# A depthwise convolution split into even and odd columns, and low parts of weights moved from GpSimd to VectorE

## The chip, the core and the metric

The kernel runs on one core of a Trainium2 chip. The metric is the device time of one execution in microseconds; the median of three runs of the kernel before is 1464.91 us (1461.34 to 1465.78). TensorE multiplies matrices, VectorE and GpSimd work element by element, ScalarE applies functions, and SyncE issues the transfers from and to device memory. In the profile they are PE, DVE, POOL, ACT and SP.

## What is computed

One layer of a streaming encoder on 1024 positions of 1024 channels, all in fp32: a convolution branch and a stick-breaking attention branch, both from one input projection, merged by sigmoid gates, an output projection, and a SwiGLU feed-forward part. The change lies in the convolution branch:

```python
u = jax.nn.glu(conv_in, axis=-1)                       # 512 channels: value times sigmoid of gate
u = causal_depthwise_conv(u, conv_dw_w, conv_dw_b)     # 31 taps along the positions, one filter per channel
u = jax.nn.silu(layernorm(u, conv_ln_g, conv_ln_b))    # normalised over the channels
conv_out = jnp.einsum('bsc,cd->bsd', u, w_conv_branch) + b_conv_branch
...
merged = jax.nn.sigmoid(g_conv) * conv_out + jax.nn.sigmoid(g_att) * att_out
mix = jnp.einsum('bsd,de->bse', merged, w_out)
```

## The kernel before

**Matmuls in two parts.** Every fp32 matrix is split into a high part, rounded to the type that TensorE multiplies in one pass, and a low part, the rest. A product is three matmuls: high by high, high by low, low by high. `load_w` (lines 64 to 72) does it for a tile of weights: SyncE loads the raw tile into one of two buffers, ScalarE makes the high part `wh` (line 70), and GpSimd subtracts it from the raw tile for the low part `wl` (line 71). A few early calls name another engine for the subtraction. `dense_T` (lines 82 to 90) makes one product of 128 output channels by 512 positions: first the matmuls with the high weights (lines 77 and 78), then those with the low weights (line 80).

**The convolution.** Channels lie on the 128 partitions and positions run along the free dimension, so the 512 channels are four blocks. `load_glu` clears the first 30 columns of a tile `u`; `glu_chunk` makes half of its 1024 positions: for "g" ScalarE writes the sigmoid of the gate into it, for "a" VectorE multiplies the value, read from PSUM, by it. `dw_ops` (lines 444 to 464) lists the work of one block: one pass over 1024 columns that multiplies by the first tap and adds the bias (`first`), 30 passes that each add one more tap (`tap`, line 453), and a sum over blocks on GpSimd (`total`, line 459).

**The order of work.** Up to the feed-forward part the program is a list, and a planner lays out each engine's queue from it when the program is built: of what is ready by its reckoning it takes what comes first in the program. On the chip each queue runs in that order. Line 505 writes the order of the mixing stage: "t" is a gate of the attention branch and the product that it gates, "g" and "a" are gate and value of a convolution block (2 and 3 here; 0 and 1 were made during attention), "c" is a gate of the convolution branch. `next_w` loads the weights of a step when the step before it begins, into two pairs of buffers; `next_branch` does it for the narrower weights of the branch products. `pump(n)` issues n steps of the convolution, alternately from the two oldest blocks that are not done, after each half of a step; `pump(1000)` issues what is left. Eight PSUM banks serve the products; a product of "t" keeps its bank until VectorE has multiplied it by the gate (line 541). Eight tiles `sgt` hold gates.

Behind the convolution (lines 574 to 613) the channel mean comes from a matmul with a constant matrix `avg` (`spread`, line 563), then squares, variance, and the normalised value in high and low parts `yH` and `yL`. TensorE makes the first "c" gates meanwhile. The convolution branch's products follow (`conv_out`), the merge is split into parts, and the output projection (lines 662 to 684) begins with eight weight tiles loaded through the two raw buffers.

Of the kernel before, what the change touches and what calls it, by code (L numbers as in the profile page):

```python
# [7 lines left out]
F32 = mybir.dt.float32  # L8
# [3 lines left out]
ALU = mybir.AluOpType  # L12
# [3 lines left out]
P = 128  # L16
S = 1024
# [3 lines left out]
HALF = 512  # L21
CONV_W = 31
NCB = 4
# [4 lines left out]
SGT = 8  # L28
# [4 lines left out]
VG, VF, VLG, VLB, VDB, VBB = 0, 8, 16, 20, 24, 28  # L33
# [4 lines left out]
def layer_kernel(ctx, tc, x, vecs, dww, gains, ident_d, mask_d, wv, wi, wbr, wo, wu, wdq, wd, out):  # L38
# [3 lines left out]
    def pool(name, bufs=1, **kw):  # L42
        return tc.tile_pool(name=name, bufs=bufs, reuse_waits="tile", **kw)
# [17 lines left out]
    hH = big.tile([P, NK, S], F32R, name="hH")  # L61
    hL = big.tile([P, NK, S], F32R, name="hL")

    def load_w(src, pl=None, bufs=2, n=1024, sub=None):
        pl = pl or wst
        raw = wst.tile([P, 1024], F32, name="wraw", tag="wraw", bufs=2)[:, 0:n]
        SP.dma_start(out=raw, in_=src)
        wh = pl.tile([P, n], F32R, name="wh", tag="wh", bufs=bufs)
        wl = pl.tile([P, n], F32R, name="wl", tag="wl", bufs=bufs)
        A.activation(out=wh, in_=raw, func=AF.Copy)  # L70
        (sub or G).tensor_tensor(out=wl, in0=raw, in1=wh.bitcast(F32), op=ALU.subtract)  # L71
        return wh, wl

    def mm3(ps, steps, first=True, last=True):
# [282 lines left out]
    us = []  # L357

    def load_glu(cb, what):
        wts[what] = load_w(wi[{"g": 4, "a": 0, "t": 28}[what] + cb])  # L360
        if what == "g":
            u = w4("u")
            G.memset(u[:, 0:CONV_W - 1], 0.0)
            us.append(u)

    def glu_chunk(cb, what, c, bank):
        ps = bank("psg")
        dense_T(wts[what], c, ps)
        dst = us[cb][:, CONV_W - 1 + c * HALF:CONV_W - 1 + (c + 1) * HALF]
        if what == "g":  # L370
            A.activation(out=dst, in_=ps, func=AF.Sigmoid)
        else:
            V.tensor_tensor(out=dst, in0=ps, in1=dst, op=ALU.mult)
# [55 lines left out]
    def bank(nm):  # L429
        return ps8.tile([P, HALF], F32, name=nm, tag="d")  # L430

    with pool("mix") as mp:
        ones = mp.tile([P, P], F32, name="ones")
        avg = mp.tile([P, P], F32, name="avg")
        G.memset(ones, 1.0)
        G.memset(avg, 1.0 / 512.0)
        attHL = []
        accs = []
        merged = []
# [1 line left out]
        turn = [0]  # L441
        csums = []

        def dw_ops(cb):
            acc = arp.tile([P, S], F32, name="acc", tag="ar", bufs=4)
            accs.append(acc)
            u = us[cb]

            def first():
                V.tensor_scalar(out=acc, in0=u[:, 0:S], scalar1=dw[:, cb, 0:1], scalar2=vec[:, VDB + cb:VDB + cb + 1], op0=ALU.mult, op1=ALU.add)  # L450

            def tap(kk):
                V.scalar_tensor_tensor(out=acc, in0=u[:, kk:kk + S], scalar=dw[:, cb, kk:kk + 1], in1=acc, op0=ALU.mult, op1=ALU.add)  # L453

            def total():
                if cb == 1:
                    csums.append(w4("csum")[:, 0:S])
                if cb in (1, 2):
                    G.tensor_tensor(out=csums[0], in0=accs[0] if cb == 1 else csums[0], in1=acc, op=ALU.add)

            ops = [(first, ())]
            for kk in range(1, CONV_W):
                ops.append((tap, (kk,)))
            dwq.append(ops + [(total, ())])

        def pump(n):
# [31 lines left out]
        def gate_sig(w, c):  # L498
            pg = bank("pg")
            dense_T(w, c, pg)  # L500
            sgt = mp.tile([P, HALF], F32, name="sgt", tag="sgt", bufs=SGT)
            A.activation(out=sgt, in_=pg, func=AF.Sigmoid)
            return sgt

# [17 lines left out]
        for pr in range(4):  # L522
            att_split(pr)
            if pr < 2:
                dw_ops(pr)
                pump(2)
        for kind, j in order:
            if kind == "c":
                break
            if (kind, j) == ("t", 2):  # L530
                pump(12)
            w = next_w()
            if kind == "t":
                w2 = next_branch()
                mg = mp.tile([P, S], F32, name="mg", tag="mg", bufs=8)
                for c in range(2):
                    cs = slice(c * HALF, (c + 1) * HALF)
                    sgt = gate_sig(w, c)
                    pb = bank("pb")
                    dense_T(w2, c, pb, attHL, 4)  # L540
                    V.tensor_tensor(out=mg[:, cs], in0=pb, in1=sgt, op=ALU.mult)
                    pump(8)
                merged.append(mg)
            else:
                wts[kind] = w
                for c in range(2):
                    glu_chunk(j, kind, c, bank)
                    pump(4)
                if kind == "a":
                    dw_ops(j)  # L550
        pump(1000)
# [28 lines left out]
        for cb in range(NCB):  # L580
# [4 lines left out]
            A.activation(out=sq, in_=accs[cb], func=AF.Square)  # L585
            sqs.append(sq)
            if cb == 1:
                G.tensor_tensor(out=sqs[1], in0=sqs[0], in1=sqs[1], op=ALU.add)
        V.tensor_tensor(out=sqs[3], in0=sqs[2], in1=sqs[3], op=ALU.add)
        V.tensor_tensor(out=sqs[3], in0=sqs[1], in1=sqs[3], op=ALU.add)  # L590
        gate_half(0, 1)
# [637 lines left out]
```

## Time and profile before

| | |
|---|---|
| median of three runs | 1464.91 us |
| the profiled execution | 1465.04 us |
| its span, from the first to the last instruction | 1463.2 us |
| mean granted clock of TensorE | 0.984 of full speed |
| TensorE busy | 1374.1 us, 94% |
| VectorE busy | 1057.3 us, 72% |
| ScalarE, GpSimd busy | 528.6 us and 282.3 us |

Shares of busy time are averages over stages that have different limits. The attention runs to about 350 us, the mixing stage with the convolution to about 690, the output projection and its norms to about 810, and the feed-forward part fills the rest. A granted clock of 1.00 is 2.4 GHz and 0.50 is 1.2 GHz. Durations of consecutive instructions on VectorE overlap a little, so that the pitch from start to start is shorter than the length of one.

### The profile page before, as it was taken

Reading aid. Unit: us, or ns where it says so; the run is one execution under the profiler, and the core shown is the slowest. Engines: PE = TensorE matmul, PEld = TensorE weight load, DVE = VectorE, ACT = ScalarE, POOL = GpSimd, SP = SyncE. Lnnn points to the kernel's source line nnn. Section 1 sums busy time; section 2 is a strip of 40 time slices with the busy share of each in tenths; the row PEclk is TensorE's granted clock in tenths of the full one; section 3 lists DMA queues with packets and bytes.
Section 4 is the critical chain, followed back from the end, with each engine's and each line's share of the span. In section 5 each row is a group of like instructions: output and inputs, shape, how many; then the busy total and the mean of one; then the engine's idle time right before and its main releaser. Section 6 shows DMA issues by size and latency. Waiting matters only on the chain.

```text
span 1463.2 us, 17209 instructions
## 1 busy us (share of the span) xinstructions
PE 1374.1 (94%) x6412; PEld 1126.8 (77%) x6412; DVE 1057.3 (72%) x1385; ACT 528.6 (36%) x863; POOL 282.3 (19%) x301
## 2 busy tenths in 40 slices
PE   6988998998999979999999799999999998999987
PEld 6866787777888757887787588888888887888875
DVE  5498878776999996325348899888877785644564
ACT  5466656553111104323325223222222222633450
POOL 2134323332324232322306200000000000000130
PEclk9999999999999989999999899999999999999999
DMA  6001001101111110212522155444444445965273
GB/s 221 23 26 40 22 23 32 42 30 36 45 49 52 43 44 22 65 43 81 172 87 94 65 198 184 174 157 158 143 149 162 166 137 178 371 230 177 89 272 100
DMA packets 62403, 160.97 MB, mean 110 GB/s; under 512 B 6384, under 2 KB 17904, under 8 KB 62320
## 3 DMA queue, kind: packets, MB, share of 16 engines
q1 hardware_dynamic: 62032, 158.83, 32.2%
q8 instruction: 50, 0.82, 0.2%
q10 hardware_dynamic: 288, 1.05, 0.2%
q14 instruction: 33, 0.27, 0.1%
HBM read 117.65 MB, written 40.11 MB: 108 GB/s over the span
## 4 chain that ended last, share of the span: by engine, by line
PE 66%; DVE 22%; issue 5%; ACT 3%; DMA 2%; POOL 2%; SPq 0%; DVEq 0%; POOLq 0%; ACTq 0%
PE m L914 28%; PE md L914 12%; DVE acc L453 11%; PE pg L77 2%; PE pg L78 2%; PE pg L80 2%; DVE R L260 2%; DVE R L255 2%; PE po L670 1%; PE po L669 1%; PE po L668 1%; DVE aL L321 1%; DVE R L257 1%; PE av L291 1%; PE pb L78 1%
## 5 line engine op out<-in xcount | busy, mean ns | idle before, releaser
L71 POOL TENSOR_TENSOR wl<-wraw,wh 128x1024 fp32r<-128x1024 f32 (+1 forms) x58 | 141.0, 2438 | 248.7 <-ACT wh L70 145.7
L453 DVE SCALAR_TENSOR_TENSOR acc<-u,dw,acc 128x1024 f32<-128x1024 f32 x120 | 176.9, 1531 | 0.3
L914 PE MATMUL m<-t,wh 128*128 128x512 f32 x528 | 134.8, 397 | 4.4 <-ACT wh L914 3.0
L914 PE MATMUL m<-hH,wh 128*128 128x512 f32 x328 | 130.6, 398 | 8.8 <-ACT wh L776 8.8
L914 PE MATMUL md<-wl,wh 128*128 128x512 f32 x308 | 122.5, 398 | 9.5 <-DVE wl L914 9.5
L914 PE MATMUL m<-hL,wh 128*128 128x512 f32 x328 | 129.9, 396 | 0.0
L914 PEld LDWEIGHTS m<-t,wh 128*128 128x128 f32 x528 | 100.0, 190 | 29.0 <-ACT wh L914 3.4
L914 PE MATMUL md<-wh 128*128 128x512 f32 x308 | 122.0, 396 | 0.0
L914 ACT ACTIVATE c<-c 128x512 f32<-128x512 f32 x44 | 27.8, 633 | 244.4 <-DVE c L914 244.4
L914 POOL TENSOR_TENSOR dc<-dc,gpo 128x512 f32<-128x512 f32 x4 | 5.1, 1301 | 541.4 <-ACT junk L914 541.4
L70 ACT ACTIVATE wh<-wraw 128x1024 fp32r<-128x1024 f32 (+1 forms) x60 | 56.5, 945 | 144.4 <-PE pg L78 50.7
L77 PE MATMUL pg<-hH,wh 128*128 128x512 f32 x256 | 101.5, 396 | 0.0
L78 PE MATMUL pg<-hL,wh 128*128 128x512 f32 x256 | 100.0, 391 | 0.0
L914 PE MATMUL md<-wh,wl 128*128 128x512 f32 x308 | 98.8, 395 | 0.0
L914 PE MATMUL m<-hH,wl 128*128 128x512 f32 x328 | 89.2, 393 | 0.0
L914 PEld LDWEIGHTS m<-hH,wh 128*128 128x128 f32 x328 | 62.2, 190 | 23.7 <-ACT wh L776 9.2
L914 PEld LDWEIGHTS md<-wl,wh 128*128 128x128 f32 x308 | 58.9, 191 | 24.5 <-DVE wl L914 11.8
L914 DVE TENSOR_TENSOR wl<-ra,wh 128x1024 fp32r<-128x1024 f32 (+1 forms) x42 | 48.4, 1153 | 38.1 <-ACT wh L914 38.0
L914 PEld LDWEIGHTS m<-hL,wh 128*128 128x128 f32 x328 | 62.2, 190 | 14.1
L914 PEld LDWEIGHTS m<-hH,wl 128*128 128x128 f32 x328 | 61.6, 188 | 14.3
L914 PE MATMUL m<-t,wl 128*128 128x512 f32 x264 | 70.7, 390 | 0.0
L914 DVE TENSOR_TENSOR u<-m,u 128x512 f32<-128x512 f32 x66 | 45.4, 688 | 33.5 <-PE m L914 32.1
(226 smaller groups left out, 3303.2 us busy)
## 6 DMA issues: line engine op xcount, KB each, us to landing
ra<-act SPq DMA_DIRECT2D x35, 512.0 KB, 6.8
wraw<-in_wi SPq DMA_DIRECT2D x32, 512.0 KB, 3.5
rg<-in_wu SPq DMA_DIRECT2D x23, 512.0 KB, 4.4
ru<-in_wu SPq DMA_DIRECT2D x22, 512.0 KB, 5.3
q<-in_wdq SPq DMA_DIRECT2D x22, 512.0 KB, 6.1
wsum<-q SPq DMA_DIRECT2D x22, 512.0 KB, 2.6
act<-sa SPq DMA_DIRECT2D x44, 256.0 KB, 2.7
rb<-wsum SPq DMA_DIRECT2D x20, 512.0 KB, 8.7
```

What stands on the lines that cost most here:

```text
L70: A.activation(out=wh, in_=raw, func=AF.Copy)
L71: (sub or G).tensor_tensor(out=wl, in0=raw, in1=wh.bitcast(F32), op=ALU.subtract)
L77: PE.matmul(ps, lhsT=lh, rhs=rh, start=(first and j == 0), stop=False)
L78: PE.matmul(ps, lhsT=lh, rhs=rl, start=False, stop=False)
L80: PE.matmul(ps, lhsT=ll, rhs=rh, start=False, stop=(last and j == n - 1))
L255: V.tensor_tensor_scan(out=R[:, 3:3 + n][:, ::-1], data0=d, data1=d, initial=1.0, op0=ALU.mult, op1=ALU.bypass)
L257: V.tensor_tensor(out=R[:, 4:3 + n], in0=sg[:, 0:n - 1], in1=R[:, 4:3 + n], op=ALU.mult)
L260: V.tensor_tensor_scan(out=R[:, 4:4 + n][:, ::-1], data0=d, data1=d, initial=carry, op0=ALU.mult, op1=ALU.bypass)
L291: PE.matmul(av, lhsT=vt[j][:, hh, :], rhs=aL[:, jj, :], start=False, stop=(j == 2 * m + 1))
L321: V.tensor_tensor(out=flat[1][:, 0:n * P], in0=tpf, in1=flat[0][:, 0:n * P].bitcast(F32), op=ALU.subtract)
L453: V.scalar_tensor_tensor(out=acc, in0=u[:, kk:kk + S], scalar=dw[:, cb, kk:kk + 1], in1=acc, op0=ALU.mult, op1=ALU.add)
L914: return lambda *a, **k: tc.keep_in_program_order(fn(*a, **k))
```

## The change

**The convolution.** `u` is kept as two halves, the even columns and the odd ones, each with its own cleared part, and `glu_chunk` writes them so, reading PSUM by every second column. With even and odd taps as two filters, three half-length filters make both halves of the output: the even taps on the even columns (16 taps, `p0`), the odd taps on the odd columns (15, `p1`), and the sums of neighbouring taps (`dws`, made once) on the sums of neighbouring columns (16). The even outputs are `p0` shifted plus `p1`; the odd ones are the third product less the first two. Per block that is 47 half-length taps and three further half-length sums (`middle`) where 31 passes over 1024 columns were. The partial sums `p0` and `p1` live in the ring of the `sgt` tiles, and the numbers of `pump` are one and a half times what they were.

**The low parts.** From the mixing stage on `load_w` subtracts on VectorE, also for the output projection's weights. The sums of `total` and of the squares go from GpSimd to VectorE. The matrix `avg` takes the place of the attention mask.

```diff
-        (sub or G).tensor_tensor(out=wl, in0=raw, in1=wh.bitcast(F32), op=ALU.subtract)
+        (sub or low_of[0]).tensor_tensor(out=wl, in0=raw, in1=wh.bitcast(F32), op=ALU.subtract)
...
-            G.memset(u[:, 0:CONV_W - 1], 0.0)
+            G.memset(u[:, 0:15], 0.0)
+            G.memset(u[:, HALF + 15:HALF + 31], 0.0)
...
-        dst = us[cb][:, CONV_W - 1 + c * HALF:CONV_W - 1 + (c + 1) * HALF]
+        ps = ps.rearrange("p (m two) -> p two m", two=2)
+        dst = us[cb].rearrange("p (two m) -> p two m", two=2)[:, :, 15 + c * 256:15 + (c + 1) * 256]
...
+    low_of[0] = V
     with pool("mix") as mp:
...
+        avg = mask
...
+        V.tensor_tensor(out=dws[:, :, 0:15], in0=dw[:, :, 0:30:2], in1=dw[:, :, 1:31:2], op=ALU.add)
+        V.tensor_copy(out=dws[:, :, 15:16], in_=dw[:, :, 30:31])
...
-            u = us[cb]
...
-            def first():
-                V.tensor_scalar(out=acc, in0=u[:, 0:S], scalar1=dw[:, cb, 0:1], scalar2=vec[:, VDB + cb:VDB + cb + 1], op0=ALU.mult, op1=ALU.add)
...
-            def tap(kk):
-                V.scalar_tensor_tensor(out=acc, in0=u[:, kk:kk + S], scalar=dw[:, cb, kk:kk + 1], in1=acc, op0=ALU.mult, op1=ALU.add)
+            ue, uo = us[cb][:, 0:HALF + 16], us[cb][:, HALF + 16:S + 32]
+            p0, p1 = [mp.tile([P, HALF + 4], F32, name=nm, tag="sgt", bufs=SGT) for nm in ("p0", "p1")]
...
+            def tap(to, u, w, k, last=None):
+                n = to.shape[1]
+                if k == 0:
+                    V.tensor_scalar(out=to, in0=u[:, 0:n], scalar1=w, scalar2=None, op0=ALU.mult)
+                else:
+                    V.scalar_tensor_tensor(out=to if last is None else last, in0=u[:, k:k + n], scalar=w, in1=to, op0=ALU.mult, op1=ALU.add)
...
+            def middle():
+                V.scalar_tensor_tensor(out=ev, in0=p0[:, 0:HALF], scalar=bias, in1=p1, op0=ALU.add, op1=ALU.add)
+                V.scalar_tensor_tensor(out=p1, in0=p0[:, 1:HALF + 1], scalar=bias, in1=p1, op0=ALU.subtract, op1=ALU.add)
+                V.tensor_tensor(out=uo[:, 0:HALF + 15], in0=uo[:, 0:HALF + 15], in1=ue[:, 1:HALF + 16], op=ALU.add)
+                V.scalar_tensor_tensor(out=p1, in0=uo[:, 0:HALF], scalar=dws[:, cb, 0:1], in1=p1, op0=ALU.mult, op1=ALU.subtract)
...
-                    G.tensor_tensor(out=csums[0], in0=accs[0] if cb == 1 else csums[0], in1=acc, op=ALU.add)
+                    V.tensor_tensor(out=csums[0], in0=accs[0] if cb == 1 else csums[0], in1=acc, op=ALU.add)
...
+            for k in range(16):
+                ops.append((tap, (p0, ue, dw[:, cb, 2 * k:2 * k + 1], k)))
+                if k < 15:
+                    ops.append((tap, (p1, uo, dw[:, cb, 2 * k + 1:2 * k + 2], k)))
+            ops.append((middle, ()))
+            for k in range(1, 16):
+                ops.append((tap, (p1, uo, dws[:, cb, k:k + 1], k, od if k == 15 else None)))
...
-                pump(2)
+                pump(3)
...
-                pump(12)
+                pump(18)
...
-                    pump(8)
+                    pump(12)
...
-                    pump(4)
+                    pump(6)
...
-                G.tensor_tensor(out=sqs[1], in0=sqs[0], in1=sqs[1], op=ALU.add)
+                V.tensor_tensor(out=sqs[1], in0=sqs[0], in1=sqs[1], op=ALU.add)
```

## Rows read from the trace of the kernel before

**Rows 1.** The page's busy times: us (share of the span) xinstructions.

```profile
PE 1374.1 (94%) x6412; PEld 1126.8 (77%) x6412; DVE 1057.3 (72%) x1385; ACT 528.6 (36%) x863; POOL 282.3 (19%) x301
```

**Rows 2.** The page's chain that ended last, share by engine.

```profile
PE 66%; DVE 22%; issue 5%; ACT 3%; DMA 2%; POOL 2%; SPq 0%; DVEq 0%; POOLq 0%; ACTq 0%
```

**Rows 3.** TensorE's waits from 350 to 560 us: total us, times, longest.

```profile
PE sp L563 <- DVE csum L576: 6.8, 1, 6.8
PE pb L77 <- DVE mg L541: 6.4, 1, 6.4
PE pb L78 <- DVE attL L482: 2.2, 2, 1.5
```

**Rows 4.** Windows: stretch, its us, busy us (xcount) by engine, granted clock, DMA share, GB/s.

```profile
516.00:521.10 5.10, 5.10 (x13) 3.99 (x14) 5.10 (x5) 0.63 (x1) 0.00 (x0) 0.52 0.00 0
549.86:555.10 5.24, 5.24 (x9) 2.84 (x10) 4.46 (x8) 0.70 (x1) 0.00 (x0) 0.51 0.00 0
600.00:686.00 86.00, 86.00 (x381) 71.18 (x380) 34.65 (x44) 21.08 (x33) 17.70 (x10) 1.00 0.21 61
```

**Rows 5.** Groups of VectorE, 352 to 550 us: busy us, mean ns | idle before.

```profile
L453 DVE SCALAR_TENSOR_TENSOR acc<-u,dw,acc 128x1024 f32<-128x1024 f32 x120 | 176.9, 1531 | 0.3
L541 DVE TENSOR_TENSOR mg<-pb,sgt 128x512 f32<-128x512 f32 x14 | 9.5, 677 | 0.0
```

**Rows 6.** Groups of GpSimd, 350 to 550 us.

```profile
L71 POOL TENSOR_TENSOR wl<-wraw,wh 128x1024 fp32r<-128x1024 f32 x13 | 41.1, 3162 | 81.6 <-PE pg L80 55.1 <-ACT wh L70 26.5
L71 POOL TENSOR_TENSOR wl<-wraw,wh 128x512 fp32r<-128x512 f32 x9 | 19.3, 2146 | 6.0 <-ACT wh L70 5.8 <-issue 0.3
```

**Rows 7.** VectorE in order of time: start us, us, line, operation, count [idle before].

```profile
353.13 1.23 DVE L482 TENSOR_TENSOR attL<-ar,attH 128x1024 fp32r<-128x1024 f32 x1 [0.20 <-ACT attH L481]
377.55 9.64 DVE L453 SCALAR_TENSOR_TENSOR acc<-u,dw,acc 128x1024 f32<-128x1024 f32 x8
538.63 3.30 DVE L453 SCALAR_TENSOR_TENSOR acc<-u,dw,acc 128x1024 f32<-128x1024 f32 x1
```

**Rows 8.** GpSimd in order of time, the same columns.

```profile
538.27 2.59 POOL L71 TENSOR_TENSOR wl<-wraw,wh 128x1024 fp32r<-128x1024 f32 x1 [2.54 <-ACT wh L70]
```

**Rows 9.** VectorE in order of time at the end of the kernel.

```profile
1387.40 0.75 DVE L914 SCALAR_TENSOR_TENSOR du<-du,pr,x1r 128x512 f32<-128x512 f32 x1 [1.65 <-POOL pr L914]
1388.07 0.74 DVE L914 SCALAR_TENSOR_TENSOR dc<-dc,pr,x1r 128x512 f32<-128x512 f32 x1
```

**Rows 10.** The chain that ended last, in order of time: start us, us, what.

```profile
545.08 1.30 DVE acc L453
546.40 1.30 DVE acc L453
```

**Rows 11.** Windows, the stretch of the first output products.

```profile
686.00:712.00 26.00, 22.42 (x87) 16.82 (x86) 2.28 (x5) 8.30 (x12) 14.23 (x6) 0.93 0.57 181
```

**Rows 12.** TensorE's waits from 560 to 830 us.

```profile
PE po L670 <- POOL wl L71: 3.0, 2, 1.7
```

**Rows 13.** Groups of GpSimd, 686 to 712 us.

```profile
L71 POOL TENSOR_TENSOR wl<-wraw,wh 128x1024 fp32r<-128x1024 f32 x6 | 14.2, 2386 | 19.8 <-ACT wh L70 19.8
```

**Rows 14.** TensorE in order of time: the fourth block's first low-weight matmuls.

```profile
428.62 1.98 PE L80 MATMUL psg<-hH,wl 128*128 128x512 f32 x8
439.50 1.98 PE L80 MATMUL psg<-hH,wl 128*128 128x512 f32 x8
```

**Rows 15.** TensorE in order of time, where the attention product waits.

```profile
358.92 0.39 PE L77 MATMUL pg<-hH,wh 128*128 128x512 f32 x1
362.60 0.50 PE L78 MATMUL pb<-attL,wh 128*128 128x512 f32 x1 [1.47 <-DVE attL L482]
```

**Rows 16.** Operations on the gate tile: duration ns min/median/max, first and last start.

```profile
L373 DVE TENSOR_TENSOR u<-psg,u x8: 676/686/693, 302.7 to 465.2; 128x512 f32<-128x512 f32 x8
```

**Rows 17.** VectorE in order of time, end of the normalisation.

```profile
590.27 2.58 DVE L612 TENSOR_TENSOR yL<-sy,yH 128x1024 fp32r<-128x1024 f32 x1 [1.63 <-ACT yH L611]
```

**Rows 18.** TensorE in order of time, the first convolution product.

```profile
597.46 0.39 PE L78 MATMUL pb<-yL,wh 128*128 128x512 f32 x1
```

More of the change, by code (lines that the diff above doesn't have):

```diff
@@ L62, in layer_kernel @@
     hL = big.tile([P, NK, S], F32R, name="hL")
+    low_of = [G]
     def load_w(src, pl=None, bufs=2, n=1024, sub=None):
@@ L430, in bank @@
         return ps8.tile([P, HALF], F32, name=nm, tag="d")
+    low_of[0] = V
     with pool("mix") as mp:
         ones = mp.tile([P, P], F32, name="ones")
-        avg = mp.tile([P, P], F32, name="avg")
+        avg = mask
         G.memset(ones, 1.0)
         G.memset(avg, 1.0 / 512.0)
+        dws = mp.tile([P, NCB, 16], F32, name="dws")
+        V.tensor_tensor(out=dws[:, :, 0:15], in0=dw[:, :, 0:30:2], in1=dw[:, :, 1:31:2], op=ALU.add)
+        V.tensor_copy(out=dws[:, :, 15:16], in_=dw[:, :, 30:31])
         attHL = []
@@ L446, in dw_ops @@
             accs.append(acc)
-            u = us[cb]
-            def first():
-                V.tensor_scalar(out=acc, in0=u[:, 0:S], scalar1=dw[:, cb, 0:1], scalar2=vec[:, VDB + cb:VDB + cb + 1], op0=ALU.mult, op1=ALU.add)
-            def tap(kk):
-                V.scalar_tensor_tensor(out=acc, in0=u[:, kk:kk + S], scalar=dw[:, cb, kk:kk + 1], in1=acc, op0=ALU.mult, op1=ALU.add)
+            ue, uo = us[cb][:, 0:HALF + 16], us[cb][:, HALF + 16:S + 32]
+            p0, p1 = [mp.tile([P, HALF + 4], F32, name=nm, tag="sgt", bufs=SGT) for nm in ("p0", "p1")]
+            p0, p1 = p0[:, 0:HALF + 1], p1[:, 0:HALF]
+            ev, od = [acc.rearrange("p (m two) -> p two m", two=2)[:, j, :] for j in range(2)]
+            bias = vec[:, VDB + cb:VDB + cb + 1]
+            def tap(to, u, w, k, last=None):
[9 more added lines that the diff above has]
+                V.scalar_tensor_tensor(out=p1, in0=uo[:, 0:HALF], scalar=dws[:, cb, 0:1], in1=p1, op0=ALU.mult, op1=ALU.subtract)
             def total():
@@ L458, in total @@
                 if cb in (1, 2):
-                    G.tensor_tensor(out=csums[0], in0=accs[0] if cb == 1 else csums[0], in1=acc, op=ALU.add)
-            ops = [(first, ())]
-            for kk in range(1, CONV_W):
-                ops.append((tap, (kk,)))
+                    V.tensor_tensor(out=csums[0], in0=accs[0] if cb == 1 else csums[0], in1=acc, op=ALU.add)
+            ops = []
+            for k in range(16):
[5 more added lines that the diff above has]
+                ops.append((tap, (p1, uo, dws[:, cb, k:k + 1], k, od if k == 15 else None)))
             dwq.append(ops + [(total, ())])
@@ L500, in gate_sig @@
             dense_T(w, c, pg)
-            sgt = mp.tile([P, HALF], F32, name="sgt", tag="sgt", bufs=SGT)
+            sgt = mp.tile([P, HALF + 4], F32, name="sgt", tag="sgt", bufs=SGT)[:, 0:HALF]
             A.activation(out=sgt, in_=pg, func=AF.Sigmoid)
```

## The prediction

> **What bounds the kernel now.** I read the busy times first, because they say which engine has room. TensorE is at work for 94% of the span and VectorE for 72% [rows 1]. So the whole kernel belongs to TensorE, and this change, which touches no matmul, can only give back time in which TensorE stands still or runs slowly. The chain that ended last is the second view: 22% of it is VectorE [rows 2], far more than an average would suggest, so there must be a stage where VectorE sets the pace. The list of what TensorE waited for finds it. Between 350 and 560 us it lost 6.8 us before the spread of the mean, waiting for the channel sum, 6.4 us before an attention-branch product that waited for VectorE to empty a bank, and 2.2 us for the low parts of the attention output [rows 3]. The two long waits cost more than their length. Directly behind them the granted clock is 0.52 and 0.51, that is the lower level of 1.2 GHz. The 13 matmuls of the first slow stretch took 5.10 us, where 381 at full clock took 86.00 us, 0.226 each, or 2.9 us for 13: a loss of 2.2. By the clock alone it would be 0.48 of 5.10, 2.4; the second, 5.24 us at 0.51, loses 2.6 so counted, and I take 2.4 [rows 4].
>
> What VectorE does there is the convolution: 120 taps of 1531 ns, 176.9 us [rows 5]. Eight of them standing alone run in 9.64 us, 1.20 each, but one that falls beside a GpSimd subtraction takes 3.30 us [rows 7, 8]. So some 33 us of the 176.9 are not arithmetic but time lost beside GpSimd, which makes the low parts of the weights at the same moment (13 wide ones at a mean of 3.2 us, 9 narrow ones at 2.1, [rows 6]).
>
> **The change part by part, against the profiled execution's own 1465.04 us (span 1463.2 and 1.84 around it; the median of the runs, 1464.91, is the same within 0.2 us).**
>
> *The convolution.* Per block of 128 channels 31 full passes go and 50 half-length ones come: 47 taps, of which two are plain multiplications, and three further sums. The nearest row for a half tap is the same operation on 512 columns at the end of the kernel: 0.75 us long, the next one starting 0.67 us later [rows 9]. I take 0.665 for the pitch, all 50 alike, 33.2 us a block against 37.2 for 31 passes at 1.20. Four blocks: 133 us. The alternation of two blocks and of the two partial sums hides that a tap needs the one before it. In the last 15 taps of the third and of the fourth block nothing is left to alternate with: there a full tap has a pitch of 1.32 instead of 1.20 [rows 10], so 30 times 0.12 or 3.6 us come on top. The Trainium skill, "VectorE: DVE Perf Modes", section on the TRN2 errata, speaks against the cut: an instruction that reads SBUF pays a fixed latency, and short tiles pay it more often. By its formula for two fp32 tensors, an estimate, a half pass is 0.69 us and the convolution 138 us. The trace shows the same thing as a pitch of 0.67 where half of 1.20 would be 0.60, so most of that price is in my sum already.
>
> *The low parts, moved to VectorE.* On VectorE a subtraction of that width takes 1.23 us [rows 7], 1.15 in a row, a narrow one 0.61 (from 0.68, [rows 5], with the same overlap). From 350 to 550 us that is 13 times 1.15 and 9 times 0.61, 20.4 us, and two channel totals, 2.3 us. GpSimd has nothing large left there, so the 33 us of slowing go.
>
> *The sum for VectorE* up to the channel sum: 133 + 3.6 + 20.4 + 2.3, 16 products and 4 gates at 0.61 (12.2), 4 attention low parts (4.6) and the sum itself (1.2): 177 us. It begins at 353.1 [rows 7] and would end at 530. TensorE reaches the spread at 549.9 less 6.4, 6.8, 2.2 of slow clock and about 1 of the 2.2 for the attention low parts: 533.5. VectorE is then 3 us early instead of 6.8 us late. Both long waits go, with what follows them: 8.6 + 9.2 = 17.8 us, and 1.0 for the attention low parts (0 to 2.2).
>
> *The output weights.* From 686 to 712 us TensorE idles 3.6 us and runs at a mean clock of 0.93 [rows 11]; 3.0 us of waiting are for GpSimd's low parts [rows 12], six of them at 2.39 us [rows 13], in a chain of load, high part, low part that reuses two buffers three times. VectorE has nothing else to do there. Each low part is 1.2 us shorter, three in a row 3.6 us. I take 3.0, between 0 (the transfers set the pace) and 5.4 (all idle time and 3.6 us at half clock, 1.8).
>
> *The new wait.* A low part now stands in VectorE's queue behind the taps issued before it. Count that queue for the weights of the fourth block's gate and value stage (the last g and a of the order t, t, g, a, t, g, a): all 96 steps of blocks one and two are issued before the third t. So the low part of g waits for 353.1 + 4.6 + 2 x 33.2 + five wide (5.8) + two narrow (1.2) + four products and two gates (3.7) = 434.8, while TensorE has the first matmul that needs it at 428.6: 6 us late. Behind it stand 24 taps of the third block (16.0), a narrow one, two products, a total and the low part of a (4.1): 455, where TensorE is at 439.5 [rows 14]: 15 us late in all, of which 9 are new. What can cover it are the matmuls with high weights of the following chunks, 16 each, 3.6 us; four of them are free of the wait, 14.5 us. The queues are laid out in advance, and in the trace the planner does such a thing: while an attention product waits 1.47 us for its low part, matmuls of the next gate chunk stand ahead of it [rows 15]. So I put 4 us for what is not covered, between 0 and 15 plus twice 2.3 for the slow clock, 20 us. From there on VectorE gains on TensorE. A low part may also have to wait itself, for its high part and for the buffer that TensorE frees, with taps and products queued behind it; since it comes late as it is, I put nothing for that.
>
> *Edits at nothing.* Two short clears for one, the small sum of taps, the reuse of the mask's tile: all off the path. The gate reads PSUM by every second column: no row shows such a read. The eight products there take 686 ns [rows 16]; no fewer columns are read, which excludes a gain, so the bounds are 0 and a doubling, 5.5 us, and I take 0, since the number of elements stays. Here the Trainium skill, "Advanced Engine Details and Errata", section Memory Cachelines, says otherwise: PSUM is read in pieces of two fp32 values and accesses that are not contiguous are slowed (it says so of matmuls); by that the upper end holds, and no run here shows it yet. In the normalisation VectorE gets about four low parts more, 4.6 us; the last low part of its output ends at 592.9 [rows 17] and is needed at 597.5 [rows 18], so 4.6 us of cover, just enough, and the slowing beside GpSimd goes there too.
>
> Sum: 1465.0 - 17.8 - 1.0 - 3.0 + 4 = 1447.2. I forecast **1447 us**, 1.2% faster.
>
> **Rivals.** *The low parts starve TensorE* where the planner does not cover them: 20 us lost instead of 4, so 1463. For it: the 15 us follow from counting. Against it: the order in [rows 15], and eight banks for the covering chunks. *Slower:* the half taps have no overlap, a pitch of 0.75 (their length in [rows 9]) instead of 0.665, as each waits for the end of the one before, and the low parts are not covered. Then 96 steps take 8 us more, the low part of g is 14 us late and that of a 25, later weights about 5 more, and with 5 for the clock TensorE loses 35 us: 1465 - 21.8 + 35 = 1478. It decides from where the loss passes 21.8 us, a pitch of about 0.67 to 0.68 with nothing covered. Against it: a full tap, 1.27 long, has a pitch of 1.20 today, and the two partial sums alternate. *The strided gate read is twice as slow:* 8 x 0.69 on VectorE, which is on the path in both places: 1453. *Everything goes*, the small waits too: 1439. *It does not do what it says*, half passes costing like full ones: the row of 0.75 speaks against it.
>
> **How the numbers follow.** Forecast case (1441 to 1455) 0.58; starved 0.20 (1455 to 1467); slower 0.10; strided read 0.07; everything 0.05. The range 1439 to 1463 holds the first, the fourth, most of the fifth and some two thirds of the second, about 0.8. What this kernel's runs can tell from no change is about 0.3%, 4.4 us. Faster than 1460.5: 0.58 + 0.07 + 0.05 and a part of the second, 0.78; within: 0.10; slower: the third and the edge of the second, 0.12.
>
> **What would show it.** The taps: some 190 half-length ones near 0.75 us each, none near 2 us. The waits for the channel sum and the bank: gone. GpSimd: nothing wide between 350 and 712 us. The output stage: no wait on GpSimd. Against me: a wait of TensorE for a low part between 425 and 465 us of more than 5 us, a gate product over 1 us, or a clock near 0.5 in a new place.

## The result and the profile after

The changed kernel takes 1442.93 us, the median of four runs (1440.8 to 1447.73), against 1464.64 of the kernel before on the same chip: a ratio of 0.986, with a 95% interval of 0.983 to 0.989. The forecast was 1447. The profiled execution is the slowest of the four, 1447.73 us with a span of 1445.9; the other three lie between 1440.8 and 1443.2. That execution is taken apart first, and the 4.8 us by which it stands above the median are told of further down.

Busy times of the changed kernel, to be read against [rows 1]:

```profile
PE 1371.8 (95%) x6412; PEld 1127.8 (78%) x6412; DVE 1044.4 (72%) x1509; ACT 529.2 (37%) x863; POOL 169.8 (12%) x259
```

TensorE issues the same 6412 matmuls. VectorE is as busy as before although it does GpSimd's work as well; GpSimd has lost 112 us. The averages would hardly tell that anything happened. The chain that ended last, by engine, says more: VectorE's share is 18% and was 22% [rows 2].

```profile
PE 72%; DVE 18%; issue 3%; ACT 3%; DMA 1%; POOL 1%; SPq 0%; DVEq 0%; POOLq 0%; ACTq 0%
```

What TensorE waits for between 340 and 720 us (total us, times, longest):

```profile
PE psg L82 <- DVE wl L73: 1.3, 1, 1.3
PE pb L80 <- DVE attL L509: 1.2, 1, 1.2
PE av L293 <- DVE aL L323: 1.0, 1, 1.0
PE psg L79 <- ACT wh L72: 0.8, 1, 0.8
PE pg L82 <- DVE wl L73: 0.3, 1, 0.3
```

The 6.8 us for the channel sum and the 6.4 us for a bank [rows 3] are gone, the 3.0 us for GpSimd's output weights [rows 12] too. Three small waits are new: 1.3 and 0.3 us for low parts that VectorE makes, 0.8 us for a high part. The windows (stretch, its us, busy us and count of PE, PEld, DVE, ACT, POOL, granted clock, DMA share, GB/s) show no slow clock left where 0.52 and 0.51 stood [rows 4], and an output stage in which TensorE is never idle, where it had worked 22.42 of 26 us [rows 11]:

```profile
350.00:425.00 75.00, 72.80 (x327) 59.41 (x326) 72.67 (x110) 16.75 (x24) 0.00 (x0) 1.00 0.13 39
425.00:455.00 30.00, 27.88 (x122) 22.43 (x121) 30.00 (x45) 3.31 (x5) 0.16 (x2) 1.00 0.12 36
455.00:540.00 85.00, 84.71 (x372) 69.54 (x371) 71.77 (x104) 15.22 (x22) 0.00 (x0) 1.00 0.20 65
674.00:700.00 26.00, 26.00 (x114) 21.03 (x113) 11.75 (x14) 9.56 (x17) 1.61 (x3) 1.00 0.60 212
```

VectorE's groups from 352 to 545 us (busy us, mean ns | idle before), and GpSimd's two largest from 560 to 760 us:

```profile
L469 DVE SCALAR_TENSOR_TENSOR p<-u,dw,p 128x513 f32<-128x513 f32 x60 | 46.1, 790 | 0.0
L469 DVE SCALAR_TENSOR_TENSOR p<-u,dw,p 128x512 f32<-128x512 f32 x56 | 42.8, 787 | 0.0
L469 DVE SCALAR_TENSOR_TENSOR p<-u,dws,p 128x512 f32<-128x512 f32 x56 | 41.4, 788 | 0.2
L73 DVE TENSOR_TENSOR wl<-wraw,wh 128x1024 fp32r<-128x1024 f32 x13 | 16.3, 1256 | 5.0 <-PE pg L82 4.7 <-ACT wh L72 0.2
L73 DVE TENSOR_TENSOR wl<-wraw,wh 128x512 fp32r<-128x512 f32 x9 | 6.4, 722 | 0.1
```

```profile
L107 POOL TENSOR_TENSOR pr<-pv,mhalf 128x1 f32<-128x1 f32 x13 | 7.4, 575 | 190.6 <-DVE pv L105 162.6 <-DVE pv L103 28.1
L804 POOL TENSOR_TENSOR wl<-rg,wh 128x1024 fp32r<-128x1024 f32 x2 | 5.8, 2913 | 0.0
```

No tap is near the 1531 ns of [rows 5], and the low parts that took GpSimd 3162 and 2146 ns [rows 6] take VectorE 1256 and 722.

**Where the 17.3 us of span came from.** I compare the start of the same matmul in both traces.

| first or last matmul | before | after | change |
|---|---|---|---|
| first gate product of the mixing stage | 351.4 | 354.3 | +2.9 |
| first spread of the mean | 549.9 | 539.4 | -10.5 |
| second spread | 572.4 | 559.4 | -13.0 |
| last convolution product | 682.8 | 669.8 | -13.0 |
| last output product | 782.5 | 763.2 | -19.3 |
| last product of the feed-forward part | 1455.4 | 1438.1 | -17.3 |

So the convolution with the normalisation behind it gains 15.9 us and the output stage 6.3. The attention ahead of it, which the change doesn't touch, is 2.9 us late here, and the feed-forward part gives back 2.0.

### The profile page after: what moved, and what is told of

It reads as the page before. It is cut to its first block, busy times and chain, and to the rows that moved or that the text cites. A ratio compares the mean times of both kernels' runs of the same rounds, so it can differ in the third digit from the quotient of the medians.

```text
span 1445.9 us, 17263 instructions
## 1 busy us (share of the span) xinstructions
PE 1371.8 (95%) x6412; PEld 1127.8 (78%) x6412; DVE 1044.4 (72%) x1509; ACT 529.2 (37%) x863; POOL 169.8 (12%) x259
## 4 chain that ended last, share of the span: by engine, by line
PE 72%; DVE 18%; issue 3%; ACT 3%; DMA 1%; POOL 1%; SPq 0%; DVEq 0%; POOLq 0%; ACTq 0%
PE m L941 28%; PE md L941 12%; DVE p L469 7%; PE pg L82 3%; PE pg L79 3%; PE pg L80 3%; PE po L697 2%; PE po L695 2%; PE po L696 2%; DVE R L262 2%; PE pb L82 1%; DVE R L257 1%; PE pb L79 1%; PE pb L80 1%; PE av L293 1%
## 5 line engine op out<-in xcount | busy, mean ns | idle before, releaser
L80 PE MATMUL pg<-hL,wh 128*128 128x512 f32 x256 | 99.7, 389 | 0.0
L73 DVE TENSOR_TENSOR wl<-wraw,wh 128x1024 fp32r<-128x1024 f32 (+1 forms) x45 | 46.7, 1049 | 48.5 <-ACT wh L72 36.7
L469 DVE SCALAR_TENSOR_TENSOR p<-u,dw,p 128x513 f32<-128x513 f32 (+1 forms) x116 | 80.2, 789 | 0.0
L941 PEld LDWEIGHTS m<-hH,wl 128*128 128x128 f32 x328 | 61.7, 188 | 14.4
L941 PEld LDWEIGHTS md<-wh 128*128 128x128 f32 x308 | 59.3, 193 | 12.8 <-ACT wh L941 0.3
```

Of the source, the lines that this page charges most:

```text
L73: (sub or low_of[0]).tensor_tensor(out=wl, in0=raw, in1=wh.bitcast(F32), op=ALU.subtract)
L80: PE.matmul(ps, lhsT=lh, rhs=rl, start=False, stop=False)
L469: V.scalar_tensor_tensor(out=to if last is None else last, in0=u[:, k:k + n], scalar=w, in1=to, op0=ALU.mult, op1=ALU.add)
L941: return lambda *a, **k: tc.keep_in_program_order(fn(*a, **k))
```

## The experiments

Each ratio is to the kernel before, run on the same chip beside it.

**One half of the change without the other.** The convolution alone: the changed kernel with its low parts of weights on GpSimd again.

```
-    low_of[0] = V
+    low_of[0] = G
```

> The changed kernel with the weights' low parts left on GpSimd everywhere; the half-length convolution stays. In the changed kernel VectorE's queue from the attention's end to the channel sum takes 168.8 us (355.9 to 524.7). Without 22 low parts (20.4 us) and with the slowing beside GpSimd as before (about 30 us) it takes 178 and ends near 534, where TensorE arrives at 537 to 539. Theory (the sum of VectorE's queue decides): the waits for a bank and for the channel sum stay away or come to 3 us at most, the output stage gives its 6 us back: 1447 us, 1444 to 1452. Rival (the slowing beside GpSimd decides, and the halved taps suffer as much from it): the waits come back, 1455 or more.

Measured: 1454.37 us (1451.92 to 1454.65), ratio 0.992 (0.990 to 0.994). The 1447 was wrong, though the channel sum is ready 4.5 us before its spread, much as expected, and the output stage gives back 5.3 us (98.7 us from the last convolution product to the last output product, 93.4 in the changed kernel). What was missed lies ahead of the spread: the stage up to it takes 190.2 us and 185.1 in the changed kernel. TensorE waits 2.9 us for low parts of the attention and 2.1 us for a bank there, and the granted clock is 0.66 from 360 to 370 us and 0.83 from 510 to 520. The rival has the time (1455), but its wait for the channel sum does not come. TensorE's waits from 340 to 790 us, two of VectorE's groups and one of GpSimd's:

```profile
PE pb L80 <- DVE attL L509: 2.9, 3, 1.2
PE po L697 <- POOL wl L73: 2.3, 2, 1.7
PE pg L79 <- DVE mg L568: 2.1, 1, 2.1
```

```profile
L469 DVE SCALAR_TENSOR_TENSOR p<-u,dw,p 128x513 f32<-128x513 f32 x60 | 49.4, 842 | 0.0
L473 DVE SCALAR_TENSOR_TENSOR p<-p,vec,p 128x512 f32<-128x512 f32 x4 | 7.7, 1926 | 0.0
```

```profile
L73 POOL TENSOR_TENSOR wl<-wraw,wh 128x1024 fp32r<-128x1024 f32 x13 | 63.5, 4883 | 98.8 <-PE pg L82 76.1 <-ACT wh L72 19.5 <-PE pb L82 3.2
```

The means hide a few long instructions: the difference of the two partial sums, a half pass, takes 1.93 us on average. From the first gate product to the end of the channel sum it is 185.7 us here and 170.4 in the changed kernel. Of these VectorE is at work 182.2 and 168.9 us, although 18.1 us of low parts (11 wide, 9 narrow) and two products (1.2 us) are not on it here. So GpSimd's work costs VectorE 13.3 + 19.3, some 33 us, as much as it cost the full taps. GpSimd suffers as well: 4883 ns for a subtraction that takes 2386 where VectorE has little to do [rows 13].

The low parts alone: the kernel before, with its low parts from the mixing stage on and its two GpSimd totals on VectorE.

```
-        (sub or G).tensor_tensor(out=wl, in0=raw, in1=wh.bitcast(F32), op=ALU.subtract)
+        (sub or low_of[0]).tensor_tensor(out=wl, in0=raw, in1=wh.bitcast(F32), op=ALU.subtract)
...
+    low_of[0] = V
...
-                    G.tensor_tensor(out=csums[0], in0=accs[0] if cb == 1 else csums[0], in1=acc, op=ALU.add)
+                    V.tensor_tensor(out=csums[0], in0=accs[0] if cb == 1 else csums[0], in1=acc, op=ALU.add)
...
```

> The kernel before with only the low parts and the sums of blocks and squares moved to VectorE; the convolution has its 31 full passes. Theory (the sum of the queue decides): four blocks of 37.2 us, 149, and 44 us for the rest make 193 us where 196 are today, so the convolution ends no earlier, a wait for the channel sum or a bank of some 7 us stays, and the low parts of the fourth block's gate and value come 17 and 30 us late with 14 us of matmuls to cover them; the output stage gains 6 us: 1463, from 1457 to 1472. Rival (the slowing beside GpSimd was the whole loss): 33 us go from the queue, both waits vanish, 1446 to 1450.

Measured: 1459.62 us (1457.93 to 1460.51), ratio 0.996 (0.994 to 0.998). The time lies in the range of the theory, but not for its reason: the channel sum is not waited for, since it is ready 12.0 us before its spread. The waits are others:

```profile
PE psg L82 <- DVE wl L73: 9.9, 1, 9.9
PE pg L82 <- DVE wl L73: 3.4, 1, 3.4
```

```profile
L456 DVE SCALAR_TENSOR_TENSOR acc<-u,dw,acc 128x1024 f32<-128x1024 f32 x120 | 147.1, 1280 | 0.1
```

Full taps without GpSimd beside them take 1280 ns, 29.8 us less than in [rows 5]. That is the loss which the prediction had put at 33. But the low parts now queue behind long taps, and TensorE waits 13.3 us for them. By medians the halves give 10.8 and 5.5 us, both together 21.7: 5 us more than the sum. Each half removes what the other one suffers from. The shorter taps let the low parts through, and the low parts off GpSimd leave the taps alone. The sums of `total` and of the squares are on VectorE in both halves, so what they are worth alone is not shown.

**The output stage.** The changed kernel with the eight output weights' low parts on GpSimd.

```
+                    low_of[0] = G
                     for k in range(2):
                         wos.append(load_w(wo[k]))
+                    low_of[0] = V
...
+    low_of[0] = G
     for k in range(2, NK):
         load_o(k)
```

> The changed kernel with the low parts of the eight output weights on GpSimd again, all else as changed. If the 6.3 us that the output stage gained come from the engine that makes the low parts (1.2 us shorter each, three in a row, and no slowing of the merge beside them): 1446 to 1449. If they come from the merge of the branches that ends earlier for other reasons: below 1445, and no wait of TensorE for a low part in that stage.

Measured: 1448.37 us (1447.07 to 1448.91), ratio 0.988 (0.986 to 0.990). TensorE's waits from 560 to 790 us begin with

```profile
PE po L699 <- POOL wl L73: 2.5, 3, 1.3
```

From the last convolution product to the last output product it is 97.0 us here, 93.4 in the changed kernel and 99.7 before. So 3.6 of the 6.3 us are the engine that makes the low parts. The other 2.7 us came without it. ScalarE's first two high parts of these weights start 2.9 us after the last convolution product begins and had started 5.3 after it (first fence: the changed kernel; second: the kernel before, where it begins at 682.8). A reason that fits is that VectorE finishes the merge sooner when nothing runs beside it:

```profile
672.72 2.00 ACT L72 ACTIVATE wh<-wraw 128x1024 fp32r<-128x1024 f32 x2
```

```profile
688.06 1.99 ACT L70 ACTIVATE wh<-wraw 128x1024 fp32r<-128x1024 f32 x2
```

The 2.4 us agree with the 2.7. Two runs bear on it. The run with the low parts alone, whose merge is undisturbed too, has 94.1 us in this stage. The convolution alone and this run both have the output weights' low parts on GpSimd and differ, for this stage, in those of the narrower weights that are made beside the merge: the high parts start 5.3 us after the last convolution product begins in the one and 3.5 in the other, and the stage takes 98.7 and 97.0 us. So 1.7 of the 2.7 us go with GpSimd's work beside the merge; the other 1.0, which the convolution alone has against the kernel before, stays open.

**How near the new wait is.** Unused half passes, added to each block between its first taps, lengthen VectorE's queue by 0.665 us each and leave the rest of the program as it is (`with_idle` issues one such pass and then the tap). Eight per block were tried first, two and four later.

```
+            def idle(k):
+                V.scalar_tensor_tensor(out=acc[:, 0:HALF], in0=ue[:, k:k + HALF], scalar=dw[:, cb, k:k + 1], in1=ue[:, 0:HALF], op0=ALU.mult, op1=ALU.add)
...
-                ops.append((tap, (p0, ue, dw[:, cb, 2 * k:2 * k + 1], k)))
+                ops.append((with_idle if k < 8 else tap, (p0, ue, dw[:, cb, 2 * k:2 * k + 1], k)))
```

> The changed kernel with eight half-length passes more per block, whose result nobody uses: 32 times 0.665, 21.3 us more in VectorE's queue, 10.6 of them before the fourth block's gate weights. In the changed kernel the channel sum is ready 14.7 us before TensorE comes to it. If only this lead counts: 6.6 us late and 2.4 for the slow clock, 1452. If the low parts behind the taps starve TensorE: the wait of 1.3 us for that low part grows to about 12, with a slow clock behind it, and the lead is not used up as TensorE is later too, 1455 to 1458. If the planner covers both: 1443 to 1446.

Measured: 1465.94 us (1463.95 to 1469.16), ratio 1.001 (1.000 to 1.002): the whole gain is gone, and every number expected was too low. The starved case was right in kind. Its two largest waits between 340 and 720 us:

```profile
PE psg L82 <- DVE wl L73: 13.1, 1, 13.1
PE pg L82 <- DVE wl L73: 8.6, 1, 8.6
```

The second one, at 514 us, nobody had expected. The lead that was to cover the loss was not touched: the channel sum is ready 16.8 us before TensorE spreads it (VectorE's sum, then TensorE's spread).

```profile
541.43 1.30 DVE L610 TENSOR_TENSOR csum<-csum,acc 128x512 f32<-128x512 f32 x2
```

```profile
559.50 1.88 PE L597 MATMUL sp<-csum,mask 128*128 128x512 f32 x4
```

To see where the loss begins, three more runs changed the dose: two and four added (`k < 2`, `k < 4`), and eight of the 16 half passes on the even columns of each block left out, so that eight taps are missing from the sum.

```
-                ops.append((tap, (p0, ue, dw[:, cb, 2 * k:2 * k + 1], k)))
+                ops.append(((lambda *a: None) if 1 <= k <= 8 else tap, (p0, ue, dw[:, cb, 2 * k:2 * k + 1], k)))
```

> The changed kernel with two half passes more per block, whose result nothing uses (8 x 0.665 = 5.3 us of VectorE in all). By the theory that VectorE's queue time goes into the time one to one, through the low parts that stand in it: 1449 us (1447 to 1451), with a wait for the low part of the fourth block's g of 1.3 + 4 x 0.665 = 4.0 us and a second wait for a low part, near 490 to 515 us, of 2 to 3. By the rival, that the loss with eight more began only at some point beyond (cover by the planner, or the 14.7 us by which the channel sum is early): 1443 to 1445, and the first wait below 2 us.

> The changed kernel with four unused half passes more per block, 10.6 us of VectorE. One to one: 1454.5 us (1452 to 1457), first wait 1.3 + 8 x 0.665 = 6.6 us, second 4 to 6. By the rival with a point from which it begins: 1443 to 1449, a bend between this run and the one with two.

> The changed kernel without eight of the first 16 half passes of each block: these taps are left out of the sum. 21.3 us of VectorE less. If what VectorE still costs here is only the waits of 1.3, 0.8 and 0.3 us, these go and nothing more: 1441 us (1440 to 1443), the spread of the mean near 537 us and the channel sum more than 30 us ahead of it. If the one to one still goes on in this direction, VectorE being the bound of the stage as before: 1422 to 1430.

With two and four more the times lie in the ranges given for one to one (1447 to 1451, 1452 to 1457), but the loss is spread otherwise than expected: the first wait is 5.2 and 7.9 us where 4.0 and 6.6 were said, the second 0.4 and 2.4 where 2 to 3 and 4 to 6 were. With eight fewer the time lies in the range of the first case (1440 to 1443).

The stage in the table is the time from the first gate product to the first spread of the mean, the lead that from the end of the channel sum to that spread. The second row is the changed kernel: its time is that of its second measurement (below), its waits, stage and lead are of the trace above. The rows come from different sets of runs, beside which the kernel before took 1465.1 to 1465.9 us.

| half passes per block | VectorE, us | median us | ratio (95%) | waits for low parts, us | stage, us | lead, us |
|---|---|---|---|---|---|---|
| 8 fewer | -21.3 | 1441.85 | 0.983 (0.982 to 0.985) | none | 181.6 | 34.0 |
| as changed | 0 | 1443.57 | 0.985 (0.983 to 0.987) | 1.3 + 0.3 | 185.1 | 14.7 |
| 2 more | +5.3 | 1449.49 | 0.989 (0.987 to 0.990) | 5.2 + 0.4 | 190.2 | 14.4 |
| 4 more | +10.6 | 1456.21 | 0.993 (0.992 to 0.994) | 7.9 + 2.4 | 197.2 | 16.8 |
| 8 more | +21.3 | 1465.94 | 1.001 (1.000 to 1.002) | 13.1 + 8.6 | 207.7 | 16.8 |

Upward every microsecond of VectorE costs one of the stage's (5.1, 12.1, 22.6 us) and one of the kernel's (5.9, 12.6, 22.4); downward 21.3 us give 3.5 of the stage, and 1.7 by medians whose ranges overlap (1440.3 to 1443.2 and 1441.8 to 1446.6). So the bend lies close to where the changed kernel stands; if the slope stays one down to it, some 3 us of VectorE below. The lead of the channel sum has no part in it: it stays at 14 to 17 us while the time rises by 22. What goes into the time is the place of the low parts in VectorE's queue. The first fence is the run with two more, the second the run with four more: the first matmuls that need the low part of the fourth block's g, with the idle time ahead in brackets.

```profile
437.55 6.18 PE L82 MATMUL psg<-hH,wl 128*128 128x512 f32 x16 [5.18 <-DVE wl L73]
```

```profile
440.48 6.80 PE L82 MATMUL psg<-hH,wl 128*128 128x512 f32 x16 [7.89 <-DVE wl L73]
```

Two to three microseconds of that price are not waiting. The same 16 matmuls take 3.94 us in the changed kernel, at a granted clock of 1.00 after 1.3 us of idleness; here they take 6.18 at a clock of 0.61 after 5.2 us, and 6.80 at 0.54 after 7.9.

**Two attempts at more.** The changed kernel again was run as a base (1443.57 us, 1441.77 to 1446.6, ratio 0.985).

> The changed kernel itself, as the measure for the three beside it: 1443 us, 1441 to 1446, ratio 0.985 to 0.987 to the kernel before.

First, the remaining GpSimd low parts at the start of the feed-forward part on VectorE.

```
-        for (h, l), src, eng in ((t2, s2, V), (t1, s1, G), (t3, s3, G)):
+        for (h, l), src, eng in ((t2, s2, V), (t1, s1, V), (t3, s3, V)):
...
-    lows = [G]
+    lows = [V]
...
-    G.tensor_tensor(out=wl2, in0=raw2, in1=wh2.bitcast(F32), op=ALU.subtract)
+    V.tensor_tensor(out=wl2, in0=raw2, in1=wh2.bitcast(F32), op=ALU.subtract)
```

> The changed kernel with the same move in the next stage: the low parts of the first feed-forward weights and operands (three groups at the start of that part, some 11 us of VectorE's time) go from GpSimd to VectorE. There VectorE is 90% busy and single operations of 0.69 us take 1.6 to 2.8 beside GpSimd, and TensorE then waits 8.9 us for a high part at the end of that chain. If the slowing beside GpSimd costs more than the added work, as it did in the mixing stage: 2 to 5 us faster than the changed kernel, 1438 to 1441. If the chain is bound by VectorE's own work: the same or up to 5 us slower.

Measured: 1442.19 us (1440.46 to 1442.49), ratio 0.984 (0.983 to 0.985), 1.4 us below the base with overlapping intervals: not told apart. The wait that it aimed at fell from 8.9 to 8.1 us only:

```profile
PE m L941 <- ACT wh L803: 8.1, 1, 8.1
```

Second, the weights of the step after the third t, the fourth block's g, loaded ahead of the 18 taps that are issued before them.

```
+            w = next_w()
             if (kind, j) == ("t", 2):
                 pump(18)
-            w = next_w()
```

> The changed kernel with the next weights asked for ahead of the 18 taps that stand before the third gate of the attention branch, so that these 18 taps no longer stand ahead of the low part of the fourth block's gate. If that place in the queue makes the wait of 1.3 us for this low part (and the 0.8 for a high part behind it): both go, 1 to 2 us faster than the changed kernel, 1441 to 1442. If the wait has another cause: the wait stays and so does the time.

Measured: 1445.94 us (1445.4 to 1447.91), ratio 0.987 (0.986 to 0.989): no gain. The waits of 1.3 and 0.8 us went, so the place in the queue did make them, but a later one took their place, with a granted clock of 0.83 in its window:

```profile
PE pg L82 <- DVE wl L73: 3.1, 1, 3.1
```

```profile
490.00:500.00 10.00, 6.92 (x24) 5.22 (x22) 10.00 (x15) 0.45 (x1) 0.00 (x0) 0.83 0.25 79
```

Both together: 1443.6 us (1441.72 to 1445.39), ratio 0.985 (0.983 to 0.987), with waits of 8.1 and 3.1 us.

> Both edits in one kernel. They lie in different stages, so that their gains should add: 1437 to 1440 if each does what is expected of it, and the better of the two alone otherwise.

No version is clearly faster than the changed kernel.

## Why the prediction held, step by step

**The two long waits (17.8 us) and the attention low parts (1.0).** Right. Both waits and the slow clock behind them are gone, and the wait for the attention's low part is 1.2 us where 2.2 stood. With the new waits taken off, the steps give 17.8 + 1.0 - 2.4 = 16.4 for the stretch, and it measured 15.9.

**The half taps.** The price was right: a pitch of 0.665 was taken, and in VectorE's order of time twelve of them run in 8.05 us, eleven pitches and one length, while one alone is 0.77 long:

```profile
374.09 8.05 DVE L469 SCALAR_TENSOR_TENSOR p<-u,dw,p 128x513 f32<-128x513 f32 x12
384.37 0.77 DVE L469 SCALAR_TENSOR_TENSOR p<-u,dw,p 128x513 f32<-128x513 f32 x1
434.46 1.27 DVE L73 TENSOR_TENSOR wl<-wraw,wh 128x1024 fp32r<-128x1024 f32 x1
454.17 1.27 DVE L73 TENSOR_TENSOR wl<-wraw,wh 128x1024 fp32r<-128x1024 f32 x1
523.41 1.29 DVE L603 TENSOR_TENSOR csum<-csum,acc 128x512 f32<-128x512 f32 x2
```

The rival in which each waits for the one before it falls with these rows. It takes the alternation to make it so: at the end of the last block, where three half passes in a row each need the one before, they run in 2.33 us, a pitch of 0.79.

**The queue of 177 us and the lead of 3.** Mis-sized. The channel sum ends at 524.7; from VectorE's first instruction of the stage at 355.9 that is 168.8 us. The plain multiplications have a pitch of 0.40, not 0.665 (8 of them, 2 us). Two products and a wide low part come after the sum, and another wide one ahead of the stretch (3.5 us). The serial ends of the blocks, counted at 0.12 per tap, were for the most part filled with other instructions (3.6 counted). With a TensorE that started 2.9 us late and came to the spread at 539.4, the lead is 14.7 us. It changed nothing in the time, since what stands next was not the lead but the low parts.

**The new wait.** The count of the queue came out closest. It put the low part of g at 434.8 and that of a at 455; VectorE started the first at 434.46 and the second at 454.17 (the third and fourth line above), after an attention 2.9 us later than the count began from, which the shorter queue made up; that it fits to 0.4 us is partly luck. The kind of cover was as argued from [rows 14, 15]: TensorE's order of time shows 32 matmuls with high weights (the first and the last stand here) before the first ones that need the low part.

```profile
427.02 0.39 PE L79 MATMUL psg<-hH,wh 128*128 128x512 f32 x1
...
434.05 0.39 PE L80 MATMUL psg<-hL,wh 128*128 128x512 f32 x1
435.78 3.94 PE L82 MATMUL psg<-hH,wl 128*128 128x512 f32 x16 [1.34 <-DVE wl L73]
440.50 0.50 PE L79 MATMUL psg<-hH,wh 128*128 128x512 f32 x1 [0.78 <-ACT wh L72]
```

The first 16 of them belong to the chunk that needs the low part and come first in any case; only the other 16, 3.6 us, are cover. So one of the following chunks covered and not four. In this execution TensorE came to the chunk 2.0 us later than before and would have needed the low part at 430.7; it ended at 435.7, 5.1 us late, 3.6 of them covered. With the 0.8 us for a high part and 0.3 us later on, 1.3 + 0.8 + 0.3 = 2.4 us were left, where 4 was taken from 0 to 20: the size was near, the count of the cover wrong. No slow clock followed.

Why no further chunk could cover is the wait for the high part in the last line. A raw buffer is free for the next load when the subtraction has read it, so the late low part held up the weights of a as well. SyncE waited 20.9 us for it, issued the load 0.03 us after its end, ScalarE made the high part at 439.38, and TensorE began with it at 440.50 (SyncE's waits in the window from 430 to 440: total us, times, longest; then SyncE and ScalarE in order of time):

```profile
SPq L69 <- DVE wl L73: 21.7, 2, 20.9
```

```profile
435.76 0.33 SPq L69 DMA_DIRECT2D wraw<-in_wi  x1
439.38 1.06 ACT L72 ACTIVATE wh<-wraw 128x1024 fp32r<-128x1024 f32 x1 [0.85 <-DMA wraw<-in_wi]
```

The prediction did not count what a late low part holds up behind it. The part on a, 9 more us late, cost nothing: the list has no wait for it, and TensorE made the next gate's products ahead of the matmuls that need it, which begin at 456.06. The rival in which the low parts starve TensorE was closer than its chance of 0.20 says. The dose runs show that the changed kernel stands at its edge, and the sentence that VectorE gains on TensorE from there on is true of the channel sum only: with eight more the low part at 514 us is late as well.

**The output weights.** Mis-sized: 3.0 taken, bounds 0 and 5.4, measured 6.3, outside them. The engine is worth 3.6, which is what three low parts of 1.2 us each in a row give. Missed was that the merge ahead of it also runs beside GpSimd in the kernel before, where the high parts start 2.4 us later; of the other 2.7 us the runs put 1.7 down to that.

**The strided gate read at nothing.** Right. The product that reads PSUM by every second column takes 706 ns (median of eight), the plain one 686 [rows 16]; the products of the attention branch, which read plainly in both kernels, drifted as far up, from a mean of 677 to 727. ScalarE's sigmoid takes 0.60 us and had taken 0.60. The Trainium skill, "Advanced Engine Details and Errata", section Memory Cachelines, says that accesses to PSUM which are not contiguous slow down matmuls. Reads by VectorE and ScalarE are not slowed here, and no run has a matmul of that kind.

**The cover of the last normalised output.** Enough, with more than before. The last low part of it ends at 577.8 and TensorE needs it at 584.5, 6.7 us of cover where [rows 17, 18] had left 4.6.

```profile
575.31 2.46 DVE L639 TENSOR_TENSOR yL<-sy,yH 128x1024 fp32r<-128x1024 f32 x2
```

**The total.** The sum was made for an execution of 1465.0 us and gave 1447.2; the profiled execution of the changed kernel took 1447.73. That agreement is partly chance, since this execution lost 2.9 us in the attention and 2.0 in the feed-forward part. There the granted clock is lower in stretches that the change leaves alone; from 120 to 140 us it is 0.92 and was 1.00:

```profile
120.00:140.00 20.00, 19.86 (x109) 16.28 (x108) 14.08 (x29) 11.85 (x24) 5.90 (x12) 0.92 0.20 51
```

It isn't the change's: the first gate product comes at 351.2 to 352.5 us in five profiles of the kernels above that hold the changed convolution, and at 353.9 to 355.0 in the six others, with the same work ahead of it; of the two kernels with the old convolution one stands on either side (351.4, 354.2). What lowers the clock there stays open. Against the median the sum is right with the two sizes put in: 1447.2, less 3.3 for the output stage and 1.6 for the new wait, plus 0.5 for the rest of the stretch, is 1442.8, and 1442.93 was measured.

## What to carry to other kernels

Where a subtraction on GpSimd runs beside a stage that VectorE sets the pace of, moving it to VectorE can shorten the stage although VectorE gets more to do; but the moved instruction then stands in a queue, so count its place there and not how early the engine is at the end of the stage, and count what its buffer holds up while it waits. Two edits that remove each other's bottleneck must be judged together: apart they gave 10.8 and 5.5 us, together 21.7. When a gain is found, add a few unused instructions and take a few away: it shows in three runs whether the kernel stands before, on or behind the bend.

## What the hardware showed

**Beside GpSimd, one of the two engines waits.** The tap of [rows 7] that begins at 538.63 beside the subtraction of [rows 8], 538.27 to 540.86, ends at 541.93, 1.07 us after it. In the run with the convolution alone it is the same with half passes (VectorE first, then GpSimd, in order of time):

```profile
519.98 2.82 DVE L475 SCALAR_TENSOR_TENSOR p<-u,dws,p 128x512 f32<-128x512 f32 x1
```

```profile
519.84 2.40 POOL L73 TENSOR_TENSOR wl<-wraw,wh 128x1024 fp32r<-128x1024 f32 x1 [13.35 <-PE pg L82]
```

The half pass ends at 522.80, 0.56 us after the subtraction at 522.24, about its own pitch. So such a pass gets hardly anything done until GpSimd is through, and halving the tap does not halve the loss: 2.1 us of the full one (3.30 against 1.20), 2.2 of the half one (2.82 against 0.66). It goes the other way too. In the same run nine half passes keep their pitch of 0.66 us beside a subtraction that lasts 8.95 us, and only a pass that begins at 410.69 is held until 0.56 us after its end at 413.02:

```profile
403.44 6.06 DVE L469 SCALAR_TENSOR_TENSOR p<-u,dw,p 128x513 f32<-128x513 f32 x9
410.69 2.89 DVE L473 SCALAR_TENSOR_TENSOR p<-p,vec,p 128x512 f32<-128x512 f32 x1
```

```profile
404.07 8.95 POOL L73 TENSOR_TENSOR wl<-wraw,wh 128x1024 fp32r<-128x1024 f32 x1 [6.41 <-ACT wh L72]
```

Waits of this kind would explain the mean of 4883 ns. What lets GpSimd in is not shown. The products of the attention branch read one operand from PSUM, and none of the 16 takes longer than 0.69 us in this run. The Trainium skill, "SBUF — State Buffer", section "SBUF: two separate sides", says that the two engines take a pair of ports as an exclusive lock for a whole instruction, where VectorE reads two operands from SBUF. These rows agree.

**The lengths drift, the pitch doesn't.** In the changed kernel half taps last 0.75 us near 366 us and 0.82 near 478, with starts 0.66 us apart in both. Sums made from lengths would have been 18% too high (0.787 against 0.665).

**What a wait costs behind it.** After 1.3 us of idleness the granted clock of the next 16 matmuls is 1.00; after 5.2 us it is 0.61 over 6.18 us, a mean of the levels of 2.4 and 1.2 GHz, and the wait costs 2.2 us more than it lasts.
